# The channel mixer's down projection as Strassen's seven half-size products, in three groups

## The chip, the cores and the metric

The kernel runs on one core of a Trainium2 chip. The metric is the device time of one execution in microseconds (us). The kernel before took 2581.75 us, the median of 3 runs (2581.56 to 2582.65). The engines are named as the profile names them: PE is TensorE, PEld its weight loads, DVE is VectorE, ACT is ScalarE, POOL is GpSimd, SP is SyncE, which issues most DMAs.

## The reference

Four layers, each a token mixer (convolution, neighbourhood attention, retention, convolution again) and then a channel mixer; before each stands an RMS norm, behind each a residual addition. The sequence has 512 tokens, the model 1024 features, the channel mixer 2816 (22 tiles of 128).

```python
def conv_ffn(h, w_up, dw_w, dw_b, w_down):
    u = dwconv(h @ w_up, dw_w, dw_b)
    val, gate = jnp.split(u, 2, axis=-1)
    return (jax.nn.gelu(gate) * val) @ w_down

for i in range(DEPTH):
    ...
    h = rmsnorm(x, norm2_g[i])
    x = x + conv_ffn(h, ffn_w_up[i], ffn_dw_w[i], ffn_dw_b[i], ffn_w_down[i])
```

The change concerns the last product, `@ w_down`: 512 tokens x 2816 features times 2816 x 1024.

## The kernel before

Everything lies transposed: features on the 128 partitions, the 512 tokens along the free axis. The residual `x` is eight tiles of 128x512 in SBUF that stay for the whole program. All matmuls are made in a split form: an operand is a high part in fp32r, made by a cast on ScalarE, and a low part, the rest, made by a subtraction on VectorE. `mm3` (L161) then makes three matmuls into one PSUM bank: high weight by high data, high by low, low by high. So each weight tile costs a DMA (`load_raw`, L146, on SyncE's queue, two buffers), a cast (L157) and a subtraction (L158; both in `split_w`, three buffers each).

The channel mixer is `ffn` (L276). Its stage has eight PSUM banks and a pool of nine 128x512 temporaries (`t512`).

- The up projection: `up(n)` makes one tile of 128 features by 512 tokens, 8 x 3 = 24 matmuls of 512 columns; tiles alternate between value and gate. There are 44 of them; the first two are made together in `up_first`.
- `mid(j, pv, pg)` (L294) takes a value tile and its gate tile: scale by the norm (L298), three taps along the tokens (ScalarE L301, VectorE L303 and L305), GELU on ScalarE (L308), the product (L309), then the split into `hh` and `hl` (cast L172, subtraction L173). All 22 results stay in SBUF.
- The down projection: for each of the eight output tiles `o`, three weight loads (8, 7 and 7 k tiles; each a DMA, a cast and a subtraction), then 22 x 3 = 66 matmuls of 512 columns, then `residual(o, ps)` (VectorE, L274) and `after(o)`. `after` is `prep` (L221) of the next stage: the cast `xh` (ScalarE, L229), the subtraction `xl` (VectorE, L232), the square (ScalarE, L245) and its sum (GpSimd, L250). In the last layer `after` stores, and the last tile is made in two halves of 256 columns.

The down projection begins when all 22 `mid` are done: the stage is an up part and then a down part. The order of the instructions on each engine is not written by hand. A planner (`TileContext` with `schedule_with_timeline_sim`) orders them when the program is built, by the order of the source and by what it expects to be ready; on the chip each engine then works through its list in order.

Of the kernel before, what the change touches and what calls it, by code (L numbers as in the profile page):

```python
# [8 lines left out]
F32 = mybir.dt.float32  # L9
F32R = mybir.dt.float32r  # L10
# [7 lines left out]
P = 128  # L18
T = 512
D = 1024  # L20
# [48 lines left out]
CORDER = (CD, 0, 1, 2, 3, 4, 5, 7)  # L69
CTAPS = (0, 3, 5, 5, 5, 5, 5, 3, 0, 0)  # L70


@with_exitstack
def tile_trunk(
# [17 lines left out]
    def nm(s):  # L92
        uid[0] += 1
        return f"{s}{uid[0]}"
# [65 lines left out]

    def mm3(o, wh, wl, ah, al, first, last):  # L161
        nc.tensor.matmul(o, wh, ah, start=first, stop=False)  # L162
        nc.tensor.matmul(o, wh, al, start=False, stop=False)  # L163
        nc.tensor.matmul(o, wl, ah, start=False, stop=last)  # L164

# [5 lines left out]
    def split(src, hi, lo, n=None):  # L171
        state["cast"] = nc.scalar.copy(hi, src)  # L172
        return nc.vector.tensor_tensor(lo, src, hi.bitcast(F32), SUB)  # L173
# [102 lines left out]
    def ffn(l, after):  # L276
        with ExitStack() as st:
            stage_pools(st, 9, 8, 0)
            hp = st.enter_context(tc.tile_pool(name=nm("ffn"), bufs=1, reuse_waits=RW))
            hh, hl = [], []  # L280
            def up(n):
# [8 lines left out]
                if n == S2[l]:  # L290
                    stats2()
                return ps

            def mid(j, pv, pg):  # L294
# [13 lines left out]
                nc.scalar.activation(acc[1], acc[1], AF.Gelu_apprx_tanh)  # L308
                nc.vector.tensor_tensor(acc[0], acc[0], acc[1], MUL)  # L309
# [3 lines left out]
                hh.append(hi)  # L313
                hl.append(lo)

# [27 lines left out]

            ups, done = up_first(), 0
            for n in range(1, 2 * FT):
                if n > 1:
                    ups.append(up(n))
                while n >= S2[l] and done < len(ups) // 2:
                    mid(done, ups[2 * done], ups[2 * done + 1])
                    done += 1  # L350
            for o in range(KD):
                ps = bank(psa if o % 2 == 0 else psb)
                ws = {}
                for k0, kn in ((0, 8), (8, 7), (15, 7)):
                    w = load_w(f_down[l, o, :, k0 * P:(k0 + kn) * P], kn * P)
                    for i in range(kn):
                        ws[k0 + i] = [t[:, i * P:(i + 1) * P] for t in w]
                if l == DEPTH - 1 and o == KD - 1:
                    for c in (slice(0, 256), slice(256, 512)):
                        for k in range(FT):  # L360
                            mm3(ps[:, c], *ws[k], hh[k][:, c], hl[k][:, c], k == 0, k == FT - 1)
                        nc.vector.tensor_tensor(x[o][:, c], ps[:, c], x[o][:, c], ADD)  # L362
                        store(o, c)
                else:
                    for k in range(FT):
                        mm3(ps, *ws[k], hh[k], hl[k], k == 0, k == FT - 1)
                    residual(o, ps)
                    after(o)

# [731 lines left out]
def _layout(inp):  # L1101
# [56 lines left out]
    for sh in range(PH):  # L1158
# [11 lines left out]
    rv = rw[:, 2048:4096].reshape(4, 2, P, 4, 512).transpose(3, 0, 2, 1, 4)  # L1170
    rout = f["ret_w_out"][0].reshape(4, 4, P, 4, 2, P).transpose(0, 3, 2, 4, 1, 5)
    arrays = {
        "xT": f["x"][0].T,
# [16 lines left out]
        "f_up": tiles(f["ffn_w_up"]),  # L1190
        "f_down": tiles(f["ffn_w_down"]),
    }
# [19 lines left out]
```

## Time and profile before

| | |
|---|---|
| median of 3 runs | 2581.75 us (2581.56 to 2582.65) |
| span of the profiled execution, first to last instruction | 2576.2 us |
| DMA | 271.78 MB, 105 GB/s in the mean |
| down projections in the profiled execution | from 453.8, 1076.5, 1878.9 and 2448.7 us |

The share of busy time of an engine is an average over stages with different limits; the windows, which give it for a stretch, say more. A row of the groups reads: line, engine, operation, what it writes and reads, shapes, count | busy us in total, mean ns of one | idle time of the engine just before them, and what ended it. A matmul's duration in a row is its latency, and successive ones overlap: what one costs is read from the distance of two starts. The span of the profiled execution is shorter than the time of a run, since it reaches from the first to the last instruction.

### The profile page before, as it was taken

How to read it: one execution, taken by the hardware profiler on the slowest of the kernel's cores; microseconds unless marked ns; L12 is line 12 of the kernel's file. 1: busy time of each engine (PE TensorE's matmuls, PEld its weight loads, DVE VectorE, ACT ScalarE, POOL GpSimd, SP SyncE). 2: the span in 40 equal slices, each digit the busy share in tenths (PEclk: the TensorE clock that was granted, in tenths of full speed). 3: DMA queues.
4: the chain of work that ended last, by engine and by line, in shares of the span. 5: the costliest groups of instructions: out<-in, count | busy, mean ns of one | idle time of the engine just before them, and what ended most of it. 6: DMA issues, size and time to landing. Idle time of an engine off the chain costs nothing.

```text
span 2576.2 us, 33719 instructions
## 1 busy us (share of the span) xinstructions
PE 2558.8 (99%) x13414; PEld 2120.2 (82%) x13414; DVE 1652.3 (64%) x2673; ACT 1050.0 (41%) x1439; POOL 258.8 (10%) x301
## 2 busy tenths in 40 slices
PE   9999999999999999999999999999999999999999
PEld 7878888889998888888888888888888888788888
DVE  7986777338877777624656566677743787677732
ACT  5554444335556444423333323444432445444421
POOL 1213000003421100000000000100000221100000
PEclk9999999999999999999999999999999999999999
DMA  6724232333332322233222221232333672222232
GB/s 241 234 86 148 90 98 88 95 103 105 97 91 71 101 95 95 90 97 110 74 85 71 84 80 58 98 99 90 97 90 97 206 222 74 90 93 95 92 107 80
DMA packets 80174, 271.78 MB, mean 105 GB/s; under 512 B 10720, under 2 KB 13664, under 8 KB 80016
## 3 DMA queue, kind: packets, MB, share of 16 engines
q1 hardware_dynamic: 73152, 256.32, 30.9%
q0 software_dynamic: 5568, 10.59, 1.7%
q10 hardware_dynamic: 1296, 2.72, 0.3%
q8 instruction: 105, 1.72, 0.3%
q14 instruction: 53, 0.43, 0.1%
HBM read 260.19 MB, written 5.63 MB: 103 GB/s over the span
## 4 chain that ended last, share of the span: by engine, by line
PE 97%; DVE 2%; ACT 0%; issue 0%; DMA 0%; SPq 0%; DVEq 0%; ACTq 0%
PE ps L164 27%; PE ps L163 27%; PE ps L162 27%; PE ps L168 3%; PE ps L169 3%; PE ps L167 3%; PE ps L485 1%; PE ps L484 1%; PE ps L483 1%; PE ps L332 1%; PE ps L333 1%; PE ps L337 1%; PE ps L724 1%; DMA x<-in_xT 0%; PE ps L539 0%
## 5 line engine op out<-in xcount | busy, mean ns | idle before, releaser
L157 ACT CAST wh<-wr 128x1024 fp32r<-128x1024 f32 (+1 forms) x410 | 423.1, 1033 | 1086.1 <-PE ps L163 775.9
L164 PE MATMUL ps<-xh,wl 128*128 128x512 f32 x1856 | 735.4, 397 | 0.1
L163 PE MATMUL ps<-xl,wh 128*128 128x512 f32 x1856 | 734.5, 396 | 0.2 <-DVE xl L232 0.2
L162 PE MATMUL ps<-xh,wh 128*128 128x512 f32 x1856 | 730.4, 394 | 0.4 <-ACT wh L157 0.4
L158 DVE TENSOR_TENSOR wl<-wr,wh 128x1024 fp32r<-128x1024 f32 (+1 forms) x407 | 494.9, 1216 | 334.4 <-ACT wh L157 332.1
L162 PEld LDWEIGHTS ps<-xh,wh 128*128 128x128 f32 x1856 | 348.5, 188 | 85.8 <-ACT wh L157 1.3
L163 PEld LDWEIGHTS ps<-xl,wh 128*128 128x128 f32 x1856 | 348.4, 188 | 85.9 <-DVE xl L232 0.5
L164 PEld LDWEIGHTS ps<-xh,wl 128*128 128x128 f32 x1856 | 348.3, 188 | 81.7 <-DVE wl L158 0.5
L162 PE MATMUL ps<-hh,wh 128*128 128x512 f32 (+1 forms) x726 | 281.6, 388 | 0.5 <-DVE x L362 0.5
L163 PE MATMUL ps<-hl,wh 128*128 128x512 f32 (+1 forms) x726 | 281.5, 388 | 0.0
L164 PE MATMUL ps<-hh,wl 128*128 128x512 f32 (+1 forms) x726 | 281.5, 388 | 0.0
L298 DVE TENSOR_TENSOR t<-ps,rstd_bc 128x512 f32<-128x512 f32 x176 | 120.8, 690 | 159.1 <-PE ps L164 159.1
L250 POOL TENSOR_TENSOR sqacc<-t,sqacc 128x512 f32<-128x512 f32 x49 | 75.1, 1533 | 1253.6 <-ACT t L245 1248.2
L162 PEld LDWEIGHTS ps<-hh,wh 128*128 128x128 f32 x726 | 136.6, 188 | 31.0 <-DVE x L362 0.7
L163 PEld LDWEIGHTS ps<-hl,wh 128*128 128x128 f32 x726 | 136.7, 188 | 30.3
L164 PEld LDWEIGHTS ps<-hh,wl 128*128 128x128 f32 x726 | 136.7, 188 | 30.3
L168 PE MATMUL ps<-wl,xh 128*128 128x256 f32 (+1 forms) x512 | 159.1, 312 | 0.5 <-DVE wl L158 0.5
L169 PE MATMUL ps<-wh,xl 128*128 128x256 f32 (+1 forms) x512 | 159.1, 312 | 0.0
L167 PE MATMUL ps<-wh,xh 128*128 128x256 f32 (+1 forms) x512 | 158.4, 312 | 0.0
L301 ACT ACTIVATE t<-t,par 128x512 f32<-128x512 f32 x176 | 142.5, 814 | 6.0 <-DVE t L298 5.8
L305 DVE SCALAR_TENSOR_TENSOR t<-t,par,t 128x511 f32<-128x511 f32 x176 | 132.0, 750 | 5.5
L303 DVE SCALAR_TENSOR_TENSOR t<-t,par,t 128x511 f32<-128x511 f32 x176 | 130.8, 744 | 0.0
(256 smaller groups left out, 3572.4 us busy)
## 6 DMA issues: line engine op xcount, KB each, us to landing
wr<-in_f_up SPq DMA_DIRECT2D x176, 512.0 KB, 3.4
wraw<-in_cdw SPq DMA_DIRECT2D x56, 608.0 KB, 5.1
wr<-in_f_down SPq DMA_DIRECT2D x64, 448.0 KB, 3.3
wr<-in_f_down SPq DMA_DIRECT2D x32, 512.0 KB, 3.5
wr<-in_cw_in SPq DMA_DIRECT2D x30, 512.0 KB, 3.9
wr<-in_nat_qkv SPq DMA_DIRECT2D x24, 512.0 KB, 3.5
wr<-in_cw_out SPq DMA_DIRECT2D x16, 512.0 KB, 3.9
wr<-in_ret_qk SPq DMA_DIRECT2D x16, 512.0 KB, 3.5
```

The source lines that it names most:

```text
L157: nc.scalar.copy(hi[:, :n], raw[:, :n])
L158: eng.tensor_tensor(lo[:, :n], raw[:, :n], hi[:, :n].bitcast(F32), SUB)
L162: nc.tensor.matmul(o, wh, ah, start=first, stop=False)
L163: nc.tensor.matmul(o, wh, al, start=False, stop=False)
L164: nc.tensor.matmul(o, wl, ah, start=False, stop=last)
L167: nc.tensor.matmul(o, ah, wh, start=first, stop=False)
L168: nc.tensor.matmul(o, ah, wl, start=False, stop=False)
L169: nc.tensor.matmul(o, al, wh, start=False, stop=last)
L298: nc.vector.tensor_tensor(u, ps, rstd_bc, MUL)
L301: nc.scalar.activation(a, u, AF.Identity, bias=pc("fdb", l * 44 + c), scale=pt[:, w + 1:w + 2])
L303: nc.vector.scalar_tensor_tensor(a[:, 1:], u[:, :T - 1], pt[:, w:w + 1], a[:, 1:], MUL, ADD)
L305: nc.vector.scalar_tensor_tensor(a[:, :T - 1], u[:, 1:], pt[:, w + 2:w + 3], a[:, :T - 1], MUL, ADD)
```

## The change

Strassen's scheme (in Winograd's form) makes the product of two 2x2 block matrices from seven block products instead of eight, at the price of sums of blocks. Here the blocks are: two output tiles (`2i`, `2i+1`), two k tiles (an even and an odd feature tile, a "pair"), and the two halves of 256 tokens. The first 20 of the 22 k tiles form ten pairs, in three groups: pairs 0 to 3, 4 to 6, 7 to 9. The last two k tiles (20, 21) are multiplied plainly, in `remainder`.

- Data: `mid` makes of each pair seven blocks of 128x256 (three stay as they are, four are sums and differences made on GpSimd), then one cast of six blocks and one with a sign on ScalarE, and two subtractions on VectorE.
- Weights: `weights(i, q)` loads the four blocks of output pair `i` and group `q` in three DMAs and makes four sums: two on GpSimd (`t`, `s3`), two on VectorE; then casts and subtractions for seven blocks instead of four. `n` is 512 columns for group 0 and 384 for groups 1 and 2.
- Products: `prod` makes one block product, 4 or 3 pairs x 3 matmuls of 256 columns. For each of the four `i` there are seven, into two PSUM banks (`xc` in one; `v` in two halves). Partial results leave `xc` by ScalarE three times; the sums with `x` are made on GpSimd and VectorE. The last two products of one `i` (`tail`) are placed inside the next `i`.
- Order: groups 0 and 1 run inside the up part, as soon as their pairs exist (after up tiles 16 and 17, and 28 and 29, with the next two up tiles as `filler` ahead of the last tail); group 2 runs at the end. `x` is added to three times.
- Pools: seven temporaries for nine; the descriptor scratch for GpSimd's DMAs is set to 8192 bytes. The weights are laid out anew on the host; their number of bytes is the same. `DMA_SUMS` is off, and its branch is left out below.

```diff
+PARTS = ((0, 4), (4, 7), (7, 10))
+PART_COL = (0, 2048, 3584, 5120)
+REST = 20
+SLOT_H = 4
+NF = 1
+NT_FFN = 7
+NWT = 2
+NWQ = 1
...
-            stage_pools(st, 9, 8, 0)
+            stage_pools(st, NT_FFN, 8, 0)
...
-                nc.vector.tensor_tensor(acc[0], acc[0], acc[1], MUL)
-                hi = hp.tile([P, T], F32R, tag=f"hh{j}", name=nm("hh"))
-                lo = hp.tile([P, T], F32R, tag=f"hl{j}", name=nm("hl"))
-                split(acc[0], hi, lo)
...
+                if j % 2 == 0:
+                    cur_f["F"] = hp.tile([P, 8, 256], F32, tag="F", name=nm("F"), bufs=NF)
+                F, b = cur_f["F"], 2 * (j % 2)
+                nc.vector.tensor_tensor(F[:, b:b + 2, :].rearrange("p a b -> p (a b)"), acc[0], acc[1], MUL)
+                gp = nc.gpsimd.tensor_tensor
+                if j % 2 == 0:
+                    gp(F[:, 4, :], F[:, 1, :], F[:, 0, :], SUB)
+                    return
+                gp(F[:, 7, :], F[:, 2, :], F[:, 4, :], ADD)
+                gp(F[:, 5, :], F[:, 2, :], F[:, 0, :], SUB)
+                gp(F[:, 6, :], F[:, 7, :], F[:, 3, :], SUB)
+                sl = (j // 2) % SLOT_H
+                hi = hp.tile([P, 7, 256], F32R, tag=f"Hh{sl}", name=nm("Hh"))
+                lo = hp.tile([P, 7, 256], F32R, tag=f"Hl{sl}", name=nm("Hl"))
+                nc.scalar.activation(hi[:, 6, :], F[:, 7, :], AF.Copy, scale=-1.0)
+                nc.scalar.copy(hi[:, :6, :], F[:, 1:7, :])
+                nc.vector.scalar_tensor_tensor(
+                    lo[:, 6, :], F[:, 7, :], -1.0, hi[:, 6, :].bitcast(F32), MUL, SUB)
+                nc.vector.tensor_tensor(lo[:, :6, :], F[:, 1:7, :], hi[:, :6, :].bitcast(F32), SUB)
...
+            def weights(i, q):
+                p0, p1 = PARTS[q]
+                n, c = (p1 - p0) * P, PART_COL[q]
+                src = f_down[l, i]
+                r1 = load_raw(src[:, c:c + 2 * n], 2 * n)
+                t = hp.tile([P, D], F32, tag="wt", name=nm("wt"), bufs=NWT)
+                s3 = hp.tile([P, T], F32, tag="ws3", name=nm("ws3"), bufs=2)
...
+                    r21 = hp.tile([P, T], F32, tag="r21", name=nm("r21"))
+                    nc.sync.dma_start(r21[:, :n], src[:, a21])
+                    nc.gpsimd.tensor_tensor(t[:, :n], r21[:, :n], r1[:, n:2 * n], ADD)
+                    nc.gpsimd.tensor_tensor(s3[:, :n], r21[:, :n], r1[:, :n], ADD)
+                sg = hp.tile([P, D], F32, tag="wq", name=nm("wq"), bufs=NWQ)
+                nc.sync.dma_start(sg[:, n:2 * n], src[:, a12])
+                w1 = split_w(r1, 2 * n, nc.vector)
+                nc.vector.tensor_tensor(t[:, n:2 * n], t[:, :n], r1[:, :n], ADD)
+                w2 = split_w(t, 2 * n, nc.vector)
...
+                nc.scalar.copy(h3[:, :n], s3[:, :n])
+                nc.vector.tensor_tensor(l3[:, :n], s3[:, :n], h3[:, :n].bitcast(F32), SUB)
+                nc.vector.tensor_tensor(sg[:, :n], t[:, n:2 * n], sg[:, n:2 * n], ADD)
...
+                nc.scalar.copy(h4[:, :2 * n], sg[:, :2 * n])
+                nc.vector.tensor_tensor(l4[:, :2 * n], sg[:, :2 * n], h4[:, :2 * n].bitcast(F32), SUB)
+                lastw = None
+                if q == len(PARTS) - 1:
...
+                    nc.sync.dma_start(r5, src[:, PART_COL[-1]:])
+                    split(r5, h5, l5)
...
+            def prod(o, w, q, b, start, stop=True):
+                p0, p1 = PARTS[q]
+                for p in range(p0, p1):
+                    s = slice((p - p0) * P, (p - p0 + 1) * P)
+                    hi, lo = H[p]
+                    mm3(o, w[0][:, s], w[1][:, s], hi[:, b, :], lo[:, b, :],
+                        start and p == p0, stop and p == p1 - 1, True)
...
+                def remainder(i, w, s12):
+                    for o, h in ((2 * i, 0), (2 * i + 1, 2)):
+                        ps = bank(psa)
+                        for k in range(REST, FT):
+                            s = slice((h + k - REST) * P, (h + k - REST + 1) * P)
+                            mm3(ps, w["rest"][0][:, s], w["rest"][1][:, s], *rest[k],
+                                k == REST, k == FT - 1)
+                        if h:
+                            nc.vector.tensor_tensor(s12, ps, s12, ADD)
+                        else:
+                            residual(o, ps)
+                            after(o)
...
+                def tail(i, w, v, s12):
+                    prod(v[:, :256], w["sg"], q, 1, False)
+                    prod(v[:, 256:], w["a12"], q, 2, True)
+                    nc.vector.tensor_tensor(x[2 * i + 1], v, s12, ADD)
+                    if final:
+                        after(2 * i + 1)
...
+                for i in range(4):
+                    w = first if i == 0 and first else weights(i, q)
+                    xb, v = bank(psa), bank(psa)
+                    xc = xb[:, :256]
+                    s12 = t512()
+                    prod(xc, w["a11"], q, 0, True)
+                    nc.scalar.copy(s12[:, 256:], xc)
+                    prod(v[:, 256:], w["a22"], q, 5, True)
+                    prod(v[:, :256], w["s1"], q, 3, True)
+                    prod(xc, w["s2"], q, 6, False)
+                    nc.scalar.copy(s12[:, :256], xc)
+                    nc.gpsimd.tensor_tensor(s12, x[2 * i + 1], s12, ADD)
+                    if prev:
+                        if final:
+                            remainder(prev[0], prev[1], prev[3])
+                        tail(*prev)
+                    prod(xc, w["s3"], q, 4, False)
+                    s3 = hp.tile([P, 256], F32, tag="sn3", name=nm("sn3"), bufs=2)
+                    nc.scalar.activation(s3, xc, AF.Copy, scale=-1.0)
+                    u2 = t512()
+                    nc.vector.tensor_tensor(
+                        u2.rearrange("p (h t) -> p h t", h=2), s3.unsqueeze(1).broadcast_to([P, 2, 256]),
+                        v.rearrange("p (h t) -> p h t", h=2), SUB)
+                    (nc.vector if final and i == 3 else nc.gpsimd).tensor_tensor(
+                        x[2 * i], x[2 * i], u2, ADD)
+                    prev = (i, w, v, s12)
+                if final:
+                    remainder(prev[0], prev[1], prev[3])
+                if filler:
+                    filler()
+                tail(*prev)
...
+            for j in range(1, FT):
+                ups_of(j)
+                if n > S2[l]:
+                    mids(j)
+                for q, (_, p1) in enumerate(PARTS[:-1]):
+                    if j == 2 * p1:
+                        w0 = weights(0, q)
+                        mids(j + 1)
+                        down(q, w0, lambda: ups_of(j + 1))
+            w0 = weights(0, len(PARTS) - 1)
+            mids(FT)
+            down(len(PARTS) - 1, w0)
...
-    nc = bacc.Bacc("TRN2", target_bir_lowering=False, num_devices=1)
+    nc = bacc.Bacc("TRN2", target_bir_lowering=False, num_devices=1, dynamic_dma_scratch_size=8192)
```

More of the change, by code (lines that the diff above doesn't have):

```diff
@@ L159, in split_w, with mm3 @@
         return hi, lo
[L161 to L164, printed above, removed]
+    def mm3(o, wh, wl, ah, al, first, last, free=False):
+        nc.tensor.matmul(o, wh, ah, start=first, stop=False, skip_group_check=free)
+        nc.tensor.matmul(o, wh, al, start=False, stop=False, skip_group_check=free)
+        nc.tensor.matmul(o, wl, ah, start=False, stop=last, skip_group_check=free)
     def mm3s(o, wh, wl, ah, al, first, last):
@@ new lines, in prod, with down @@
+            def prod(o, w, q, b, start, stop=True):
[5 more added lines that the diff above has]
+                        start and p == p0, stop and p == p1 - 1, True)
+            def down(q, first=None, filler=None):
+                final = q == len(PARTS) - 1
+                def remainder(i, w, s12):
[7 more added lines that the diff above has]
+                            nc.vector.tensor_tensor(s12, ps, s12, ADD)
+                        else:
+                            residual(o, ps)
[6 more added lines that the diff above has]
+                        after(2 * i + 1)
+                prev = None
+                for i in range(4):
[29 more added lines that the diff above has]
+                tail(*prev)
@@ L349, in ffn, with mids @@
+            ups = up_first()
+            done, n = 0, 2
+            def mids(upto):
+                nonlocal done
+                while done < upto:
                     mid(done, ups[2 * done], ups[2 * done + 1])
                     done += 1
[L351 to L368, printed above, removed]
@@ new lines, in ups_of @@
+            def ups_of(j):
+                nonlocal n
+                while n < 2 * j + 2:
+                    ups.append(up(n))
+                    n += 1
+            for j in range(1, FT):
[7 more added lines that the diff above has]
+                        down(q, w0, lambda: ups_of(j + 1))
@@ L1171, in _layout @@
     rout = f["ret_w_out"][0].reshape(4, 4, P, 4, 2, P).transpose(0, 3, 2, 4, 1, 5)
+    fd = f["ffn_w_down"].reshape(4, FT, P, 8, P)
+    macros = []
+    for i in range(4):
+        units = [fd[:, 2 * p0 + par:2 * p1:2, :, o] for p0, p1 in PARTS
+                 for o, par in ((2 * i + 1, 0), (2 * i, 1), (2 * i, 0), (2 * i + 1, 1))]
+        units += [fd[:, REST:, :, o] for o in (2 * i, 2 * i + 1)]
+        macros.append(np.concatenate(
+            [u.transpose(0, 2, 1, 3).reshape(4, P, -1) for u in units], -1))
+    fdown = np.stack(macros, 1)
     arrays = {
@@ L1190, in _layout @@
         "f_up": tiles(f["ffn_w_up"]),
-        "f_down": tiles(f["ffn_w_down"]),
+        "f_down": fdown,
     }
```

36 lines of the change are left out of this document (28 added, 8 removed).

## The prediction

> **What bounds the kernel now.** I read the page first (shares of the span, then the chain that ended last), then the windows of single stages, the waits, and last the start times of single matmuls.
>
> ```profile
> span 2576.2 us, 33719 instructions
> ...
> PE 2558.8 (99%) x13414; PEld 2120.2 (82%) x13414; DVE 1652.3 (64%) x2673; ACT 1050.0 (41%) x1439; POOL 258.8 (10%) x301
> ...
> PE 97%; DVE 2%; ACT 0%; issue 0%; DMA 0%; SPq 0%; DVEq 0%; ACTq 0%
> ```
>
> TensorE is busy 99% of the span and is 97% of the chain. A saved matmul is therefore saved time, as long as nobody else becomes late. Whether the others have room must be read by stage (columns: length, then busy us of PE, PEld, DVE, ACT, POOL):
>
> ```profile
> 60.00:100.00 40.00, 40.00 (x440) 36.11 (x439) 39.67 (x51) 21.94 (x22) 8.32 (x17) 1.00 0.72 224
> 230.00:452.00 222.00, 222.00 (x953) 178.56 (x953) 161.33 (x205) 96.23 (x123) 1.57 (x3) 1.00 0.31 101
> 453.00:577.00 124.00, 124.00 (x533) 99.75 (x532) 45.12 (x43) 42.42 (x42) 8.01 (x6) 1.00 0.32 95
> ```
>
> The second row is the up projection of layer 0, the third its down projection: VectorE is busy 73% of the one and 36% of the other. The first row, in a convolution, shows VectorE full (39.67 of 40 us) and TensorE still without a gap: the order of instructions that the planner writes keeps TensorE fed even by a full helper.
>
> ```profile
> ACT wh L157 <- PE ps L163: 775.9, 276, 15.0
> ```
>
> ScalarE's weight casts wait for matmuls to release the buffer, so weights lie ready well before they are used.
>
> **Matmuls removed and added.**
>
> ```profile
> L162 PE MATMUL ps<-hh,wh 128*128 128x512 f32 (+1 forms) x726 | 281.6, 388 | 0.5 <-DVE x L362 0.5
> ...
> 2549.80 0.39 PE L162 MATMUL ps<-hh,wh 128*128 128x512 f32 x1
> ...
> 2552.83 0.39 PE L163 MATMUL ps<-hl,wh 128*128 128x512 f32 x1
> ```
>
> These two are 13 matmuls apart: one of 512 columns takes 3.03/13 = 0.233 us, start to start (the 0.39 of the row is latency). At 256 columns, each matmul with its own weight load as in the change:
>
> ```profile
> 599.76 0.28 PE L167 MATMUL ps<-wh,xh 128*128 128x256 f32 x1
> ...
> 602.81 0.28 PE L169 MATMUL ps<-wh,xl 128*128 128x256 f32 x1
> ```
>
> 26 steps, 0.117 us each: half the columns cost half. A layer had 8 tiles x 22 x 3 = 528 matmuls of 512 columns, 123.0 us (726 rows at L162 are 4 x 176 and 22 more for the last tile's second half, which costs nothing extra). It gets 7 products x 4 row pairs x 10 k pairs x 3 = 840 of 256 columns, 98.5 us by 0.1173, and the two k tiles left over, 8 x 2 x 3 = 48 of 512, 11.2 us. That is 109.7 for 123.0: 13.3 us less a layer, 53 us for four. With nothing late this is the whole gain.
>
> **What VectorE, ScalarE and GpSimd get.**
>
> ```profile
> L158 DVE TENSOR_TENSOR wl<-wr,wh 128x1024 fp32r<-128x1024 f32 x343 | 425.0, 1239 | 232.9 <-ACT wh L157 232.4
> L158 DVE TENSOR_TENSOR wl<-wr,wh 128x896 fp32r<-128x896 f32 x64 | 69.9, 1092 | 101.5 <-ACT wh L157 99.7
> L173 DVE TENSOR_TENSOR hl<-t,hh 128x512 fp32r<-128x512 f32 x88 | 60.2, 684 | 2.7 <-ACT hh L172 2.7
> L173 DVE TENSOR_TENSOR ol<-ps,oh 64x256 fp32r<-64x256 f32 x32 | 13.2, 413 | 5.3 <-ACT oh L172 4.9
> L274 DVE TENSOR_TENSOR x<-ps,x 128x512 f32<-128x512 f32 x55 | 38.0, 691 | 122.2 <-PE ps L164 122.2
> L865 POOL TENSOR_TENSOR t<-t,t 128x512 f32<-128x512 f32 x8 | 10.3, 1293 | 298.5 <-ACT wh L157 277.0 <-DVE t L862 21.4
> L686 POOL TENSOR_TENSOR bm<-W,mask 128x256 f32<-128x256 f32 x48 | 39.7, 855 | 34.8 <-DVE sm L711 28.8 <-issue 5.5 <-DMA mask<-in_nmask 0.2
> ```
>
> Between these rows I read 0.96 us for 768 columns and 0.55 for 384 on VectorE, 1.07 for 384 on GpSimd. Each weights(i, q) gives VectorE three operations of 2n columns and three of n: 3 x 1.24 + 3 x 0.68 = 5.8 us for n = 512 (group 0), 3 x 0.96 + 3 x 0.55 = 4.5 for n = 384 (groups 1 and 2). Two additions from PSUM follow, 1.4. Group 2 adds the split of the leftover weights (0.7), two more additions (1.4) and the two prep subtractions (0.75 each, shown below). GpSimd gets two weight sums and two additions of 512: 5.2 us in group 0, 4.7 in the others, and in group 2 two additions of squares (2.6), which it had before. TensorE's time for one i is 84 x 0.1173 = 9.85 us, 63 x 0.1173 = 7.4, and 7.4 + 2.8 = 10.2. So VectorE alone takes 7.2 of 9.85, 5.9 of 7.4, 9.5 of 10.2: it fits. GpSimd alone takes 5.2, 4.7, 7.3: it fits too.
>
> ScalarE gets four casts for an i: in group 0 three of 1024 and one of 512, with three short copies out of PSUM:
>
> ```profile
> L157 ACT CAST wh<-wr 128x1024 fp32r<-128x1024 f32 x346 | 362.7, 1050 | 851.0 <-PE ps L163 544.9 <-issue 205.9 <-PE ps L169 49.9
> L172 ACT CAST hh<-t 128x512 fp32r<-128x512 f32 x88 | 54.3, 617 | 7.3 <-DVE t L309 7.3
> L620 ACT ACTIVATE qk<-ps,rstd_col 128x256 f32<-128x256 f32 x32 | 13.3, 470 | 8.2 <-PE ps L169 7.3 <-DVE rstd_col L258 0.9
> ```
>
> 3 x 1.05 + 0.62 + 3 x 0.47 = 5.2 us of 9.85: no cost.
>
> But the two helpers are not independent. In one place before, both worked on SBUF (the last row is the same VectorE operation alone):
>
> ```profile
> 196.47 2.41 POOL L158 TENSOR_TENSOR wl<-wr,wh 128x1024 fp32r<-128x1024 f32 x1 [2.15 <-ACT wh L157]
> 198.82 1.75 POOL L250 TENSOR_TENSOR sqacc<-t,sqacc 128x512 f32<-128x512 f32 x1
> ...
> 197.05 2.38 DVE L232 SCALAR_TENSOR_TENSOR xl<-x,png,xh 128x512 fp32r<-128x512 f32 x1 [0.83 <-ACT xh L229]
> ...
> 1108.13 1.09 DVE L158 TENSOR_TENSOR wl<-wr,wh 128x896 fp32r<-128x896 f32 x1
> 1109.14 0.75 DVE L232 SCALAR_TENSOR_TENSOR xl<-x,png,xh 128x512 fp32r<-128x512 f32 x1
> ```
>
> xl began at 197.05 and ended at 199.43, 0.55 us after GpSimd's operation ended at 198.88: it stood still while GpSimd ran. GpSimd's next took 1.75 for 1.29: it stood still for xl. So an operation with two SBUF inputs on one engine holds up such a one on the other. L865's 1.29 was measured beside VectorE operations that read PSUM, which do not collide. [...]
>
> So I add what collides. The last two rows also show that VectorE's operations overlap by 0.08 us (1.01 apart, 1.09 long), so I take 0.08 off each, and 0.05 off GpSimd's (198.82 - 196.47 = 2.35 for 2.41). Group 0: 5.3 + 5.0 = 10.3 of 9.85 us; group 1: 4.05 + 4.5 = 8.55 of 7.4; group 2: 6.0 + 7.0 = 13.0 of 10.2. Short by 0.45, 1.15 and 2.8 for an i, times four: 17.6 us a layer. The weights of i = 0 (7.8, 6.1 and 6.1 us: 20.0) are prepared before each group, in the up projection. Is there room? Its 27% of VectorE's 246 us are 66 us. The new half-sums take 4 x 0.86 of GpSimd (as L686) for a pair of tiles, 34 us over ten pairs, and VectorE's wider split of H (six blocks of 256 and one: 1.8 + 0.4 instead of 2 x 0.68) 8 us. 24 us remain: enough for 20.0. Against this, each group starts with one mid, of which about 4 us collide (four filter steps of 0.75, a product of 0.69, a half-sum), 12 in all; those of groups 0 and 1 can also be done after the group, since the stage has eight PSUM banks and a group holds three or four. That leaves 17.6 - 20.0 + (4 to 12) = 1.6 to 9.6 us a layer; I take the middle, 5.6, as neither end has a row nearer to it.
>
> **The start of groups 0 and 1.** The last H needed comes from the mid of two up tiles that ended 2 x 24 x 0.233 = 11.2 us earlier.
>
> ```profile
> L301 ACT ACTIVATE t<-t,par 128x512 f32<-128x512 f32 x176 | 142.5, 814 | 6.0 <-DVE t L298 5.8
> L305 DVE SCALAR_TENSOR_TENSOR t<-t,par,t 128x511 f32<-128x511 f32 x176 | 132.0, 750 | 5.5
> L308 ACT ACTIVATE t<-t 128x512 f32<-128x512 f32 x88 | 55.6, 632 | 159.6 <-DVE t L305 159.6
> ```
>
> Its chain: 0.69 (as L274) + 0.81 + 2 x 0.75 + 0.63 + 0.69, three half-sums on GpSimd 2.6, cast of H 1.5 (six blocks), split 2.2: 10.6 us, and a collision or two beyond. The first products of three k pairs (some 3 us) can go before it. I take 1 us for each start, 2 a layer; bounds 0 and 4.
>
> **Edits that I cost at nothing.** The weights' DMAs become 40 a layer for 24, of the same bytes, on SyncE's queue. The load of r21 waits for GpSimd's sums of the i before, and everything behind it in that queue, the next up tile's raw weights too, waits with it. Its loop (landing 3.3 us, sums 2.1) is 5.4 us of 7.4, so it fits unless the sums are slow. h4 and l4 have one buffer, free again when tail(i) ends; cast and split take 2.3 us and TensorE has five products, 5.3 us, before it needs them. The smaller scratch for GpSimd's DMAs lies in convolution and attention:
>
> ```profile
> wr<-in_f_down SPq DMA_DIRECT2D x64, 448.0 KB, 3.3
> ...
> POOL xf L435 <- issue: 55.4, 6, 13.3
> ```
>
> I take 0, since TensorE has no gap there; the upper bound is once that longest wait, 13 us. The last store is 512 columns wide where two halves went out: under 1 us later.
>
> **The sum.** A layer: -13.3 + 5.6 + 2 = -5.7; four: -23. The profiled span is 2576.2, the median of the runs 2581.75, so 5.55 us lie around the span and stay: 2581.75 - 23 = 2559.
>
> **The rivals.** *Nothing collides where it matters*: the planner places the sums under PSUM reads, as L865 lay. Loss 0 to 3 a layer: 2529 to 2541. For it speaks the convolution's full VectorE without a gap. [...] If nothing is gained by preparing ahead, the loss is 17.6 a layer and 2 at the starts, 19.6 for a gain of 13.3, so +25 us: 2607. It decides from a loss of 13.3 a layer. For it: collisions hold up VectorE's whole queue, also reads of PSUM behind them; group 2 is the worst, with the next stage's weights to split as well. Against: 24 us of room in the up projection. With 4 us at the starts it is 2615. *Close to even*: losses of 11 to 15 a layer, 2573 to 2589. That the products cost more than half is excluded by 0.117.
>
> **How the numbers follow.** Forecast (losses 3 to 11 a layer): 0.46; no collisions 0.14; near even 0.15; port-bound 0.25. A measurement tells 0.2% (5 us) from no change. Near even splits 0.02 faster, 0.09 within and 0.04 slower: faster 0.62, same 0.09, slower 0.29. The range leaves out the best part of the no-collision case below 2537 and the worst of the port-bound one above 2610, together under 0.2. The forecast's own range is 2541 to 2573.
>
> **What would show it.** PE matmuls 13414 + 4 x 360 - 66 = 14788; 256-column products 0.117 apart; GpSimd's 512-wide sums between 1.3 and 2.3 us with VectorE's splits stretched beside them; TensorE gaps mostly in group 2, waiting for weight splits or for x. It is wrong if gaps sit elsewhere (casts, DMA landings), or sum to over 13 us a layer.

## The result, and the profile after

The changed kernel takes 2643.34 us (median of 4 runs, 2641.78 to 2646.89) where the kernel before takes 2582.2 (2581.56 to 2582.95): a ratio of 1.0239, with an interval of 1.0225 to 1.0254. It is 61 us slower; 23 us faster was forecast. The page of the profiled execution after, with the mean granted clock of TensorE from the view of the cores:

```profile
span 2645.1 us, 37819 instructions
...
PE 2557.1 (97%) x14788; PEld 2186.7 (83%) x14788; DVE 2003.2 (76%) x2980; ACT 1184.3 (45%) x1695; POOL 703.4 (27%) x649
...
PE 76%; DVE 12%; issue 4%; DMA 3%; POOL 3%; ACT 2%; DVEq 0%; SPq 0%; POOLq 0%; ACTq 0%
```

```profile
core 0: 2645.1 us, clock 0.984
```

The matmuls are as many as counted, 14788. But TensorE's part of the chain that ended last falls from 97% to 76%, and VectorE's rises from 2% to 12%: TensorE now waits. Its busy time hardly fell, though it has less to do; a part of that is the clock, whose mean was 1.000 before. What it waits for, from the view of the waits (us in total, times, the longest):

```profile
PE ps L171 <- DVE t L473: 18.0, 7, 5.2
PE ps L171 <- ACT wh L166: 16.0, 6, 4.2
PE ps L172 <- DVE hl L182: 9.6, 8, 1.4
PE ps L171 <- ACT Hh L342: 7.2, 4, 2.0
PE ps L172 <- DVE Hl L345: 6.5, 4, 1.7
```

Nearly all of these are products of the down projection that wait for VectorE, or for a cast on ScalarE that itself came late.

A ledger shows where the time went. For each channel mixer (first matmul of the up projection to last of the down projection) I took the distances between matmul starts out of the trace. "Full" counts 0.2326 us for 512 columns and 0.1174 for 256; "clock" is what matmuls took more than that in stretches where the trace records the granted clock at half; "idle" is the rest. Sums over the four layers, us:

| | channel mixers | full | clock | idle |
|---|---|---|---|---|
| before | 1480.9 | 1475.0 | 0 | 5.8 |
| after | 1542.5 | 1423.2 | 23.7 | 95.8 |
| difference | +61.6 | -51.8 | +23.7 | +90.0 |

The matmuls saved what they should, 51.8 us; idle time of 22.5 us a layer and a halved clock of 5.9 a layer took more back. Idle time by place: up projection 0.7 to 0.8 a layer; group 0 5.4 to 6.6; group 1 4.5 to 5.0; group 2 15.2, 13.6, 13.8 and, in the last layer, which prepares no next stage, 6.0. (The spans differ by 68.9, the medians by 61: after's profiled execution was the slowest of its four, 2646.89 us, and 7 us lie outside the channel mixers, most of them half clock.) The gaps were forecast mostly in group 2; it has 48.6 of the 95.8 us, and groups 0 and 1 have some 43.

**How a group starts late.** VectorE's timeline in layer 0 (start, us, then the instruction), ahead of group 0:

```profile
296.68 1.78 DVE L398 TENSOR_TENSOR wt<-wt,wr 128x512 f32<-128x512 f32 x1
...
304.77 1.78 DVE L398 TENSOR_TENSOR wt<-wt,wr 128x512 f32<-128x512 f32 x1
306.47 0.74 DVE L314 SCALAR_TENSOR_TENSOR t<-t,par,t 128x511 f32<-128x511 f32 x1
...
310.13 0.68 DVE L330 TENSOR_TENSOR F<-t,t 128x512 f32<-128x512 f32 x1
310.73 1.77 DVE L314 SCALAR_TENSOR_TENSOR t<-t,par,t 128x511 f32<-128x511 f32 x1
312.53 1.64 DVE L316 SCALAR_TENSOR_TENSOR t<-t,par,t 128x511 f32<-128x511 f32 x1
314.10 1.21 DVE L398 TENSOR_TENSOR wt<-wt,wr 128x512 f32<-128x512 f32 x1
```

and GpSimd's:

```profile
310.28 1.67 POOL L394 TENSOR_TENSOR ws<-r,wr 128x512 f32<-128x512 f32 x1 [4.29 <-DVE wl L167]
311.91 1.72 POOL L393 TENSOR_TENSOR wt<-r,wr 128x512 f32<-128x512 f32 x1
313.59 1.17 POOL L335 TENSOR_TENSOR F<-F 128x256 f32<-128x256 f32 x1
```

The filter step that takes 0.74 alone takes 1.77 beside GpSimd's weight sum, a sum L398 1.78 instead of 0.68. And the order is against the start: the sums at 310.28 and 311.91 are those of a later `i`, yet they stand on GpSimd ahead of the half-sum L335 that the products of the fourth k pair wait for: VectorE had its input ready at 310.81 (L330), and it begins at 313.59. The slowed filter steps belong to the next `mid`; what made L330 late is ahead of it in VectorE's list, weight sums and splits, some of them stretched. ScalarE stands still for L335, and behind the cast of H that needs it stands in its list a weight cast:

```profile
314.79 0.42 ACT L341 ACTIVATE Hh<-F 128x256 fp32r<-128x256 f32 x1 [4.87 <-POOL F L335]
315.12 1.03 ACT L166 CAST wh<-wr 128x1024 fp32r<-128x1024 f32 x1
```

For this weight cast TensorE waits, after the products of three k pairs:

```profile
312.76 0.29 PE L173 MATMUL ps<-Hh,wl 128*128 128x256 f32 x1
316.19 0.58 PE L171 MATMUL ps<-Hh,wh 128*128 128x256 f32 x1 [3.15 <-ACT wh L166]
...
318.99 0.41 PE L171 MATMUL ps<-Hh,wh 128*128 128x256 f32 x1
319.20 0.41 PE L172 MATMUL ps<-Hl,wh 128*128 128x256 f32 x1
```

It stands for 3.15 us, and then matmuls of 256 columns are 0.21 apart. The view of the windows (length, busy us of PE, PEld, DVE, ACT, POOL, then the granted clock):

```profile
193.00:300.00 107.00, 107.00 (x465) 86.08 (x464) 76.67 (x100) 47.08 (x58) 40.24 (x46) 1.00 0.43 136
...
305.00:312.50 7.50, 7.50 (x41) 6.35 (x40) 7.50 (x8) 2.41 (x3) 3.21 (x3) 1.00 0.30 105
...
316.20:322.40 6.20, 5.66 (x25) 5.36 (x25) 4.88 (x5) 2.19 (x2) 0.56 (x1) 0.50 0.26 85
```

VectorE is busy 72% over the 107 us before group 0, but all of the 7.5 us that decide; and the clock is at 0.50 after the gap, which costs 2.3 us more.

**How group 2 ends late.** VectorE in layer 1, before the last `i`:

```profile
1230.07 1.69 DVE L167 TENSOR_TENSOR wl<-wr,wh 128x1024 fp32r<-128x1024 f32 x1
1231.68 0.68 DVE L448 TENSOR_TENSOR x<-ps,t 128x512 f32<-128x512 f32 x1
1232.29 1.15 DVE L241 SCALAR_TENSOR_TENSOR xl<-x,png,xh 128x512 fp32r<-128x512 f32 x1
1233.36 0.68 DVE L440 TENSOR_TENSOR t<-ps,t 128x512 f32<-128x512 f32 x1
1233.96 1.90 DVE L408 TENSOR_TENSOR l<-wq,h 128x768 fp32r<-128x768 f32 x1
1235.78 0.67 DVE L473 TENSOR_TENSOR t<-sn,ps 128x512 f32<-128x512 f32 x1
```

L473 reads the PSUM bank that the next products go on writing, and TensorE waits 5.15 us for it. It isn't slow itself (0.67); it stands behind a list whose operations with two SBUF inputs are stretched (1.69 for 1.21, 1.90 for 0.95), the next stage's weights among them.

### The profile page after: what moved, and what is told of

It is laid out like the page before. It is cut to its first block, busy times and chain, and to the rows that moved or that the text cites. A ratio compares the mean times of both kernels' runs of the same rounds, so it can differ in the third digit from the quotient of the medians.

```text
span 2645.1 us, 37819 instructions
## 1 busy us (share of the span) xinstructions
PE 2557.1 (97%) x14788; PEld 2186.7 (83%) x14788; DVE 2003.2 (76%) x2980; ACT 1184.3 (45%) x1695; POOL 703.4 (27%) x649
## 4 chain that ended last, share of the span: by engine, by line
PE 76%; DVE 12%; issue 4%; DMA 3%; POOL 3%; ACT 2%; DVEq 0%; SPq 0%; POOLq 0%; ACTq 0%
PE ps L172 20%; PE ps L171 20%; PE ps L173 20%; DVE wl L167 3%; PE ps L178 3%; PE ps L176 3%; PE ps L177 3%; DMA wr<-in_f_down 3%; PE ps L628 1%; POOL wt L393 1%; PE ps L626 1%; PE ps L627 1%; DVE wt L398 1%; DVE t L314 1%; DVE Hl L345 1%
## 5 line engine op out<-in xcount | busy, mean ns | idle before, releaser
L166 ACT CAST wh<-wr 128x1024 fp32r<-128x1024 f32 (+1 forms) x362 | 372.4, 1030 | 646.5 <-PE ps L172 413.8
L167 DVE TENSOR_TENSOR wl<-wr,wh 128x1024 fp32r<-128x1024 f32 (+1 forms) x359 | 465.6, 1297 | 160.6 <-ACT wh L166 159.9
L171 PE MATMUL ps<-Hh,wh 128*128 128x256 f32 x640 | 187.2, 299 | 23.8 <-ACT wh L166 14.5
L172 PE MATMUL ps<-Hl,wh 128*128 128x256 f32 x640 | 187.4, 295 | 6.5 <-DVE Hl L345 6.5
L173 PE MATMUL ps<-Hh,wl 128*128 128x256 f32 x640 | 184.7, 296 | 3.7 <-DVE wl L167 3.7
L171 PE MATMUL ps<-Hh,h 128*128 128x256 f32 x480 | 139.2, 290 | 18.0 <-DVE t L473 18.0
L171 PEld LDWEIGHTS ps<-Hh,wh 128*128 128x128 f32 x640 | 128.2, 203 | 29.5 <-ACT wh L166 15.4
L316 DVE SCALAR_TENSOR_TENSOR t<-t,par,t 128x511 f32<-128x511 f32 x176 | 145.6, 829 | 3.5
L314 DVE SCALAR_TENSOR_TENSOR t<-t,par,t 128x511 f32<-128x511 f32 x176 | 144.1, 822 | 1.6 <-ACT t L312 1.4
L172 PE MATMUL ps<-Hl,h 128*128 128x256 f32 x480 | 138.2, 288 | 0.0
```

The lines of the kernel that those rows point to most:

```text
L166: nc.scalar.copy(hi[:, :n], raw[:, :n])
L167: eng.tensor_tensor(lo[:, :n], raw[:, :n], hi[:, :n].bitcast(F32), SUB)
L171: nc.tensor.matmul(o, wh, ah, start=first, stop=False, skip_group_check=free)
L172: nc.tensor.matmul(o, wh, al, start=False, stop=False, skip_group_check=free)
L173: nc.tensor.matmul(o, wl, ah, start=False, stop=last, skip_group_check=free)
L314: nc.vector.scalar_tensor_tensor(a[:, 1:], u[:, :T - 1], pt[:, w:w + 1], a[:, 1:], MUL, ADD)
```

## The experiments

What to tell apart: whether the loss is the **collisions** of VectorE and GpSimd in SBUF, the **load** on VectorE wherever sums are made, or the **order** (starts at a fixed place, helpers' lists in order), and how much of it is the **clock**. All runs, as differences to the kernel before, timed on the same chip; idle and clock are sums over the channel mixers as above, VectorE's standing still the sum of its durations there above the shortest of each operation (before: 14.7 us; an empty field was not counted).

| | us to before | ratio, interval | idle | clock | standing still |
|---|---|---|---|---|---|
| after | +61.1 | 1.0225 to 1.0254 | 95.8 | 23.7 | 171.8 |
| e1_allvec | +22.1 | 1.0070 to 1.0100 | 64.5 | 15.1 | 32.3 |
| e2_nosums | -1.2 | 0.9985 to 1.0003 | 48.3 | 4.6 | 98.1 |
| e3_late | +43.8 | 1.0153 to 1.0183 | 79.1 | 15.0 | 169.2 |
| e4_warm | +77.7 | 1.0273 to 1.0313 | 80.1 | 17.3 | 158.2 |
| e5_dmasums | +23.3 | 1.0077 to 1.0107 | 64.4 | 15.0 | 105.8 |
| e7_dmasums_late | +24.3 | 1.0081 to 1.0111 | 58.3 | 15.5 | |
| e8_dmasums_vec_late | +13.9 | 1.0034 to 1.0067 | 48.0 | 9.1 | 31.3 |
| e9_allvec_late | -20.3 | 0.9908 to 0.9937 | 30.3 | 3.7 | 28.6 |
| e10_wsums_vec | +22.3 | 1.0072 to 1.0100 | 63.4 | 12.9 | 106.9 |
| e11_squares_vec | -20.6 | 0.9906 to 0.9933 | 26.6 | 2.8 | 21.9 |
| e12_no_xl | -27.8 | 0.9878 to 0.9905 | 24.0 | 2.3 | |
| e13_parts | -21.0 | 0.9908 to 0.9935 | 28.8 | 4.2 | 30.6 |
| e14_writes | -3.0 | 0.9978 to 0.9996 | 46.1 | 5.9 | 109.4 |
| e15_wsums_vec_late | -10.6 | 0.9941 to 0.9968 | 36.3 | 4.9 | |
| e16_parts_squares | -27.7 | 0.9872 to 0.9899 | 25.8 | 1.5 | |

**e1_allvec**: all of the new sums from GpSimd to VectorE.

```diff
-                gp = nc.gpsimd.tensor_tensor
+                gp = nc.vector.tensor_tensor
...
-                    nc.gpsimd.tensor_tensor(t[:, :n], r21[:, :n], r1[:, n:2 * n], ADD)
-                    nc.gpsimd.tensor_tensor(s3[:, :n], r21[:, :n], r1[:, :n], ADD)
+                    nc.vector.tensor_tensor(t[:, :n], r21[:, :n], r1[:, n:2 * n], ADD)
+                    nc.vector.tensor_tensor(s3[:, :n], r21[:, :n], r1[:, :n], ADD)
```

(and likewise the sums with `x`, L464 and L476)

> All additions that the change put on GpSimd (half-sums of H, two weight sums, the two additions with x) run on VectorE instead; the computation is the same. In the changed kernel VectorE stands still about 43 us a layer behind GpSimd in the channel mixers (durations above the shortest of each operation, 171.8 us over four layers), and GpSimd 29 us behind VectorE. Collision theory (the two hold each other up, and the lists lag behind what the planner expected): VectorE gets about 39 us more work a layer and loses the 43 us of standing still, so it is no slower than the changed kernel: 2600 to 2645 us, and VectorE operations are back at their undisturbed durations (512 columns 0.68, 1024 columns 1.22). Load theory (VectorE just has too much to do, collisions matter little): 39 us more on the full engine make it clearly slower: 2665 to 2710 us.

It is 39 us faster than after, at 2601.22 us in the range of the collision theory, though VectorE has all the work. Its page:

```profile
PE 2542.2 (98%) x14788; PEld 2177.9 (84%) x14788; DVE 2012.2 (77%) x3328; ACT 1183.8 (45%) x1695; POOL 260.6 (10%) x301
```

348 instructions more on VectorE, and its busy time rises from 2003.2 to 2012.2 us. Its durations in the channel mixers, less standing still, are 1292 us for 1108: 184 us of work came back, 140 us of standing still went. Of what GpSimd took off VectorE, three quarters came back as standing still. Load by itself falls as the cause of the whole loss; e10 and e16 show below where it may still count.

**e2_nosums**: the two weight sums are left out; in their place the block `a21` is loaded into both buffers, so `t` and `s3` are not the sums.

```diff
-                    r21 = hp.tile([P, T], F32, tag="r21", name=nm("r21"))
-                    nc.sync.dma_start(r21[:, :n], src[:, a21])
-                    nc.gpsimd.tensor_tensor(t[:, :n], r21[:, :n], r1[:, n:2 * n], ADD)
-                    nc.gpsimd.tensor_tensor(s3[:, :n], r21[:, :n], r1[:, :n], ADD)
+                    nc.sync.dma_start(t[:, :n], src[:, a21])
+                    nc.sync.dma_start(s3[:, :n], src[:, a21])
```

> The two weight sums on GpSimd are left out: the third block is loaded straight into both buffers instead of being added to another (so the weights of three products are not the sums). VectorE's and TensorE's own work is unchanged. Collision theory: 24 GpSimd operations of about 1.4 us a layer go, and with them about half of the standing still; TensorE's gaps fall from 20 to about 10 us a layer and the half-clock time with them: 2585 to 2605 us. Load theory: VectorE's work is the same, so 2630 to 2645 us.

62 us less than after, and 7 us below the collision theory's range: these 96 instructions carry the whole loss against before, though not the gain that was forecast, since 48.3 us of idle time stay, 32 of them in group 2. It leaves open whether it is their reading, their length or the waits for them.

**e14_writes** answers that: in place of each sum a sum of one column and two fills of the rest; waits and buffers stay. Three of the seven products have constants for most of a weight.

```diff
+                    for o, b in ((t, r1[:, 2 * n - 1:2 * n]), (s3, r1[:, :1])):
+                        nc.gpsimd.tensor_tensor(o[:, :1], r21[:, :1], b, ADD)
+                        nc.gpsimd.memset(o[:, 1:n], 0.01)
+                        nc.gpsimd.memset(o[:, 1:n], 0.02)
```

> The two weight sums stay on GpSimd as to place, waits and about length, but each is one addition of a single column, that waits for the landings, and two memsets of the rest (so the weights of three products are constants). A memset reads nothing. Collision theory: without reads there is nothing to collide with VectorE's second input; the time falls as with the sums left out: 2578 to 2592 us, and VectorE's and GpSimd's durations beside each other are the undisturbed ones. Order theory (GpSimd's list and its length delay the weights): as the changed kernel, 2625 to 2645 us.

64 us less than after, 2 from e2, and 1 us below the collision theory's range. GpSimd is occupied there about as long as by an undisturbed sum, but reads next to nothing. Its groups of instructions, and after's for the sums:

```profile
L395 POOL MEMSET ws<- 128x511 f32 x16 | 8.4, 526 | 0.0
L396 POOL MEMSET ws<- 128x511 f32 x16 | 8.4, 527 | 0.2
L394 POOL TENSOR_TENSOR ws<-r,wr 128x1 f32<-128x1 f32 x48 | 13.0, 271 | 83.0 <-DMA wr<-in_f_down 50.7 <-DVE l L405 32.2
```

```profile
L394 POOL TENSOR_TENSOR ws<-r,wr 128x512 f32<-128x512 f32 x16 | 28.3, 1771 | 29.1 <-DVE wl L167 12.8 <-DVE l L403 11.1 <-DMA wr<-in_f_down 5.2
```

0.27 + 2 x 0.53 = 1.32 us in place of 1.77 (1.29 undisturbed). And VectorE beside such fills (300.12 to 301.24) runs at its shortest:

```profile
300.08 0.69 DVE L400 TENSOR_TENSOR wt<-wt,wr 128x512 f32<-128x512 f32 x1 [0.20 <-POOL wt L394]
300.69 1.22 DVE L167 TENSOR_TENSOR wl<-wr,wh 128x1024 fp32r<-128x1024 f32 x1
```

So it is the reading of SBUF by GpSimd that costs, and not the place or the waits of these 96 instructions: for them, collisions are shown. VectorE's sum into `wt`, with two SBUF inputs, takes 0.69 us beside a fill here (L400) and 1.78 beside a GpSimd sum in after (L398 at 296.68).

**e10_wsums_vec**: of e1's edits the two weight sums alone.

> Of the changed kernel only the two weight sums move from GpSimd to VectorE (so all four are there); half-sums of H and additions with x stay on GpSimd, groups begin as in the change. All additions on VectorE gave 2601 us, the sums left out 2578. Collision theory: the weight sums are the larger part of the collisions in group 2 and at the starts; 12 us more work a layer on VectorE, some 20 us less standing still: 2600 to 2620 us. Load theory: 2650 to 2670 us.

The same time as e1 (+22.3 and +22.1), in the range of the collision theory, with 107 us of standing still left: the half-sums of H and the sums with `x` collide too, but where it costs less. Why is it 24 us behind e2? Most of it is at the starts: groups 0 and 1 idle 4.4 to 5.3 and 2.9 to 3.2 us there, 0.9 to 2.1 and 1.1 to 1.9 in e2. That fits a start that is decided by the length of VectorE's list ahead of the last `mid`, whether it is long by standing still or by work.

**e3_late** starts groups 0 and 1 two up tiles later, with nothing else changed; **e9_allvec_late** is e1 and e3 together, **e15_wsums_vec_late** e10 and e3.

```diff
-                    if j == 2 * p1:
+                    if j == 2 * p1 + 1:
                         w0 = weights(0, q)
-                        mids(j + 1)
                         down(q, w0, lambda: ups_of(j + 1))
```

> Groups 0 and 1 start one pair of up tiles later, so that the last H has 22 us instead of 11 to be made. Start theory (the chain of the last H is late, as its steps queue behind weight sums): the gaps at the two starts, about 4.5 and 4 us of 20 a layer, go, and the half clock that follows them: 10 to 14 us a layer, 2590 to 2605 us. Load theory: VectorE is full in this stretch for whatever reason, the gap comes back at another place: 2630 to 2645 us.

> All additions on VectorE (2601.22 us by itself) and groups 0 and 1 one pair later (2622.92 by itself, 20 us under the changed kernel). If the two losses are separate (group 2 by collisions, the starts by the short time for the last H), they add: 2578 to 2590 us. If the starts are late because VectorE is full, giving an engine that is fuller more time helps less: 2590 to 2601 us.

> Two weight sums moved to VectorE (2601.6 us by itself) and late starts. With all additions on VectorE and late starts it was 2558.74. If the half-sums of H and the additions with x cost nothing on GpSimd: 2553 to 2562 us. If their collisions count once the starts are free: 2566 to 2585 us.

e3 alone wins 17 us and falls between the two ranges on record: the starts fall to 2.7 to 3.5 and 3.1 to 4.8 us, group 2 keeps its 12 to 15 (6 in the last layer). e9 wins 81, which is more than e1's 39 and e3's 17 together, and better than either theory had it (2578 at the least): with both, the starts vanish (0.7 and 0.5 us), which fits a list ahead of them that is neither stretched nor late. That e9's 2558.74 us, 20 below before, is the time that was forecast for the change (2559) is chance: e9 has the sums elsewhere and starts later. Its idle time sits in group 2 (6.6 us a layer, 1.1 in the last). e15 is 10 behind e9, in the range for collisions that count: the sums that are left on GpSimd cost 2.4 us a layer.

**e4_warm** adds 66 matmuls a layer that compute nothing, to keep TensorE busy in gaps.

```diff
+                def warm(count):
+                    o, h = bank(psa), H[PARTS[q][0]][0]
+                    for _ in range(count):
+                        nc.tensor.matmul(o[:, :256], h[:, 1, :P], h[:, 0, :], start=True, stop=True)
+
+                warm((28, 14, 0)[q])
```

(and `warm(24)` ahead of the last tail of group 2)

> TensorE is given idle matmuls of 256 columns into a spare PSUM bank, where it would stand still: 28 ahead of group 0, 14 ahead of group 1, 24 around the last tail of group 2; the order of all else is the same. Clock theory (gaps of some us are followed by 3.4 or 6.8 us at half clock, 70 us in the channel mixers in all, in which matmuls of 256 columns are 0.213 apart instead of 0.12): the clock stays at 1.0 in most places and 15 to 30 us come back: 2613 to 2630 us, with the waits for VectorE still there. If the half clock costs nothing beside the gaps: 2643 to 2652 us, since the idle matmuls can only add.

17 us slower than after, beyond both ranges, and inconclusive as a test of the clock's price. The 28 ran from 310.58 to 313.9, ahead of the products that could have filled the gap; these came later, and TensorE stood 2.78 us all the same. Half clock fell only from 23.7 to 17.3 us, the added matmuls cost 66 x 0.117 = 7.7 us a layer.

**e5_dmasums, e7_dmasums_late, e8_dmasums_vec_late**: the kernel's own switch, `DMA_SUMS = True`: the two weight sums as DMAs that add, issued by GpSimd; e7 with e3, e8 with e3 and all the other sums on VectorE.

> The branch of the changed kernel that was off: the two weight sums are made by DMAs that add on landing, issued from GpSimd's queue; the computation is the same. With the sums left out (the run without sums) the time was 2577.95 us. Collision theory: a DMA holds no engine's way to SBUF, so as there, plus 24 issues a layer of about 0.57 us on GpSimd: 2578 to 2590 us, gaps at the starts of groups 0 and 1 near 1 to 2 us, group 2 still 9 to 12. Rival: the added DMA (a second transfer behind the first, 3 us each) makes the weights late: 2600 to 2640 us, with TensorE waiting for landings.

> The weight sums by adding DMAs, and groups 0 and 1 one pair later. Start theory: what is left of the starts (1 to 2 us of idle a group) goes, 4 to 10 us below the run with adding DMAs alone. Collision theory alone: the starts are already nearly free there, so no change within 4 us. In neither case does group 2 change.

> The weight sums by adding DMAs, groups 0 and 1 one pair later, and the half-sums of H and the two additions with x on VectorE instead of GpSimd: GpSimd keeps only the squares, as before the change. Collision theory: nothing of the change collides any more; VectorE has 27 us more work a layer but stands still 25 us less; group 2 falls from 9 to 12 us of idle to 5 to 7 (there it fell by as much when all additions went to VectorE): 2555 to 2572 us. Load theory: VectorE is fuller, 2585 to 2605 us.

e5 and e8 came out 12 and 21 us above the collision theory's ranges and inside those of their rivals; e7 takes e5's time within 1 us, as free starts had it. The starts are free in e5 as in e2 (0.9 to 2.3 us), and beside the adding DMAs VectorE stands still about as little (105.8 us for 98.1, and 171.8 in after), but a new wait appears. e5's waits of TensorE and of GpSimd:

```profile
PE ps L171 <- DVE t L473: 12.2, 4, 4.2
PE ps L218 <- DVE rstd_col L267: 9.5, 3, 4.0
...
POOL wt L388 <- DMA wt<-in_f_down: 88.9, 22, 32.8
```

GpSimd's issue waits in its list for the block that it adds to (up to 32.8 us), but the squares for the norm are not late by it in layer 0: the last sum of squares begins at 211.39, in after at 211.38. What holds up the norm's rstd_col there is VectorE's list:

```profile
223.31 0.62 ACT L402 CAST h<-ws 128x512 fp32r<-128x512 f32 x1 [1.58 <-DMA ws<-in_f_down]
...
223.96 0.69 DVE L403 TENSOR_TENSOR l<-ws,h 128x512 fp32r<-128x512 f32 x1 [0.65 <-ACT h L402]
...
229.10 1.23 DVE L167 TENSOR_TENSOR wl<-wr,wh 128x1024 fp32r<-128x1024 f32 x1 [0.86 <-ACT wh L166]
230.25 0.17 DVE L267 COPY rstd_col<-sm 128x4 f32<-128x4 f32 x1
```

Two splits stand among the steps of the norm and wait, by ScalarE's casts, for landings: of an added block (L403), and of weights of the up projection (L167, whose cast waited 3.14 us). rstd_col comes at 230.25, in after at 225.99, and TensorE waits 4.03 us for it. In layers 2 and 3 the same split L403 stands ahead of the norm's steps, and TensorE waits 3.0 and 2.4 us. So the rival, weights that land late, has the mechanism, by way of VectorE. In the up projection TensorE idles 1.8 to 5.2 us a layer. In e8 it also idles 6.3, 4.5 and 1.4 us behind the last product of layers 0 to 2, for VectorE's last sum with `x` (L448); this lies outside the ledger, and its cause was not sought. Each issue also occupies GpSimd for 0.9 us, and the adding transfers land 4.3 to 5.8 us later, the plain ones 2.4 to 4.3:

```profile
ws<-in_f_down SPq DMA_DIRECT2D x16, 256.0 KB, 4.3
wt<-in_f_down POOLq DMA_DIRECT2D x16, 256.0 KB, 4.8
ws<-in_f_down POOLq DMA_DIRECT2D x16, 256.0 KB, 5.8
```

**e11_squares_vec, e12_no_xl, e13_parts, e16_parts_squares** ask for the rest, group 2. e11 is e9 with the sum of squares on VectorE; e12 is e9 without the subtraction `xl` for the next stage (left out); e13 is e9 with groups of 3, 3 and 4 pairs, so that group 2 has more matmuls for the same additions; e16 is e13 and e11.

```diff
-            squares(k, src, perm)
+            squares(k, src, perm, nc.vector)
...
-PARTS = ((0, 4), (4, 7), (7, 10))
-PART_COL = (0, 2048, 3584, 5120)
+PARTS = ((0, 3), (3, 6), (6, 10))
+PART_COL = (0, 1536, 3072, 5120)
```

> All additions on VectorE and late starts (2558.74 us), and the additions of squares in every stage on VectorE too, so that GpSimd has no additions at all beside the channel mixers. Collision theory: what is left of group 2's loss (6.6 us idle and 1.4 clock in each of three layers) comes from the squares: 28 us of standing still go for 17 us more work: 2545 to 2556 us. Load theory: VectorE is 94% busy in group 2, so 17 us more work make it later: 2559 to 2572 us.

> As the run with all additions on VectorE and late starts (2558.74 us), but the low part of the next stage's input is not made in the channel mixers (the next stage reads old values there): eight VectorE operations of 0.75 to 1.3 us a layer go from group 2 and its end. Load theory for what is left: group 2 loses idle in the three layers that have such a preparation, from 6.6 to 1 to 3 us, as in the last layer (1.1): 2540 to 2549 us. If the rest is not VectorE's load but the order (the last sums come late whatever is ahead of them): 2553 to 2559 us.

> All additions on VectorE, late starts, and groups of 3, 3 and 4 pairs instead of 4, 3 and 3: group 2 then has 12.65 us of TensorE for about 10.5 of VectorE in each i, where it had 10.2 for 9.5, while groups 0 and 1 are the tighter ones. Load theory: group 2's idle falls from 6.6 to about 3, and the earlier groups, which had 0.7 and 0.5, lose 0 to 2 us: 2546 to 2560 us. If the tightness of the earlier groups decides: 2560 to 2580 us.

> Groups of 3, 3 and 4 pairs, late starts, all additions of the channel mixers and those of squares on VectorE: no collision is left. Load theory for group 2's rest: idle there falls below the 5 to 6 us that each edit alone left, to 3 to 5: 2546 to 2555 us. If the rest has another cause (the end of the stage, where the last sums and the next stage's preparation follow each other): 2556 to 2561 us, as each alone.

e11 and e13 alone change nothing that can be measured (-20.6 and -21.0 for e9's -20.3): e11 falls between its two ranges, e13 in the load theory's, though group 2 idles 6.2 us there where 3 were expected. e12 wins 7 us, between its two ranges; e16 wins 7, in the range of the load theory, and computes everything. Only both edits together help; that in e11 work comes in place of the collision, and in e13 the collision stays in the longer group, would explain it and is not shown. e16's page:

```profile
span 2547.9 us, 37636 instructions
...
PE 2519.6 (99%) x14788; PEld 2159.2 (85%) x14788; DVE 2006.7 (79%) x3370; ACT 1184.0 (46%) x1695; POOL 193.6 (8%) x259
```

VectorE is as busy as after (2006.7 and 2003.2) with 390 instructions more, and TensorE back at 99%. At 2552.24 us, ratio 0.9885 (0.9872 to 0.9899), it is the fastest complete version and beats both kernels. In group 2 4.5 us stay in layers 1 and 2, 6.8 in layer 0 and 1.2 in the last. In layer 1 the window of group 2 (columns as above) has

```profile
1133.00:1188.00 55.00, 52.20 (x384) 48.91 (x384) 50.06 (x72) 30.25 (x49) 0.00 (x0) 1.00 0.28 82
```

VectorE at 91%, which fits its load; but which of its operations must go was not settled.

## Why the prediction was wrong, step by step

- **Matmuls**, -13.3 us a layer: right. The count is exact, and the ledger has -12.9.
- **VectorE and GpSimd alone fit**: right for groups 0 and 1, where e9 has VectorE carry all the new sums and TensorE idles 1.2 us a layer; in group 2 it still idles 6.6, so there it isn't shown.
- **Collisions**: mechanism right (in after L398 takes 1.78 us beside a GpSimd sum, instead of 0.68) and so is the shortage; the step that failed is the one after it, "Is there room?", answered with "24 us remain: enough for 20.0", which brought 17.6 a layer down to the 5.6 taken. The room exists (VectorE is busy 72% in the 107 us before group 0), but it is a mean over the whole up projection. In the last 7.5 us VectorE is at 100%, with sums of later `i` in both helpers' lists ahead of the chain that group 0 waits for; and group 2 idles as if nothing had been prepared ahead: 12.2 us a layer (14.2 where a next stage is prepared) for the 2.8 x 4 = 11.2 short. The subtraction 17.6 - 20.0 was wrong before any run: it lets the 7.8 us prepared for group 0, which was short of 1.8, pay for group 2, which was short of 11.2 with 6.1 prepared. Group by group 5.1 us stay, and with the 4 to 12 of the mids the term is 9.1 to 17.1 for 5.6: on the prediction's own numbers, about even.
- **Starts of groups 0 and 1**, 2 us a layer, at most 4: mis-sized. Both groups together idle 10.7. The chain was added up from undisturbed durations with "a collision or two"; it was not asked what else stands ahead of it on VectorE and GpSimd. e9 shows 1.2 for the same matmuls, with that list cleared and the start two tiles later.
- **The clock** was in no term. Before, the granted clock was full throughout the channel mixers; after, it takes 5.9 us a layer.
- **Edits at nothing**: nothing speaks against them. None of r21, h4, the scratch or the last store stands among TensorE's larger waits; none was tried by itself.
- **The sum**: -5.7 was to come; -12.9 + 22.5 + 5.9 = +15.5 a layer came. The rival in which nothing is gained by preparing ahead ("port-bound", 0.25) had the loss and, in collisions that hold up VectorE's queue, the mechanism nearly right, 19.6 a layer for 22.5 of idle time; its 2607 lacks the clock and the larger starts. No run shows a port that the two helpers share; what the runs show is operations that stretch beside each other, by 171.8 us of VectorE's time in after and 32.3 in e1, where the sums are VectorE's. The sign that was to show the forecast wrong, gaps of over 13 us a layer, is what happened.

## What to carry to other kernels

Work moved from VectorE to GpSimd relieved VectorE by a quarter of it here: 184 us were moved and 140 came back as standing still. In after, VectorE's filter step L314, which reads SBUF alone, took 0.73 to 1.78 us, while its sums that read PSUM (L440, L448, L473) took 0.67 to 0.69 in all 112 records; beside fills in place of GpSimd's sums (e14) the sum L400 took 0.69. So cost the two helpers together, by their durations beside each other. Room on VectorE counted here only in the microseconds ahead of the instruction that the next stage waits for (busy 72% over 107 us, and all of the 7.5 that decided): read the list there, and not the share over a stage. A gap on TensorE cost more than its length here: half clock added a quarter to the idle time (23.7 us to 90), and 2.3 us to a single gap of 3.15.

## What the runs showed of the hardware that was not expected

In after, gaps on TensorE come with half clock: ahead of the span's last 2 us the trace records 15 stretches at half the granted clock, of 3.41 or 6.83 us each, and the gap that ends at 316.19 comes with one from 315.57 to 322.4. But a gap needn't do it. In the convolution of layer 0 both kernels have the same wait of 1.9 us (TensorE for VectorE's L454 or L597). The windows after it, of before and then of after:

```profile
133.00:136.50 3.50, 3.50 (x56) 3.50 (x57) 1.56 (x2) 1.60 (x2) 1.06 (x3) 1.00 0.41 141
```

```profile
134.00:137.50 3.50, 3.50 (x35) 3.50 (x36) 1.53 (x2) 0.59 (x1) 1.08 (x3) 0.60 0.44 124
```

56 matmuls lie in the one and 35 in the other, at clock 1.00 and 0.60. The traces show one difference between the two equal gaps. In after all recorded changes of the clock lie whole multiples of 3.4133 us apart, within 2 ns; before has two changes, at 6.04 and 2576.27, 753 such steps apart. Counted in these steps, the gap of 1.93 us in after lies whole inside one (131.25 to 134.67), and half clock is recorded from its end to 138.08; in before a step ends at 132.33 and splits the gap into 1.25 and 0.68. That this sets the two apart is the author's estimate from this one pair; no run moved a gap on purpose.

The other is that GpSimd's fills didn't disturb VectorE in e14 (0.69 and 1.22 us beside them, its shortest), so filling was work that GpSimd could take.
